# Strassen's product for the output projection of the second layer

## The chip, the cores and the metric

The kernel runs on one core of one Trainium2 chip. TensorE (PE) multiplies matrices, VectorE (DVE), ScalarE (ACT) and GpSimd (POOL) do the elementwise work, and SyncE (SP) issues DMAs. The metric is the device time of one execution in microseconds, as the median of several executions.

## The reference

Two decoder layers over 1024 tokens of width 1024 in float32. The first is a sliding-window attention, the second (HGRN2) a gated linear recurrence. What matters here is the end of the second layer: the recurrence's output `o` (normalised per head and scaled by `gnorm_w`) is multiplied by a SiLU gate, projected by a 1024 x 1024 matrix, normalised by rows, scaled and added to the residual.

```python
o = o.reshape(B, T, REC_WIDTH) * jax.nn.silu(z.astype(jnp.float32))
y = o.astype(h.dtype) @ w_out                    # hgrn2_mixer
...
x = x + rmsnorm(y, post_norm_w[layer])           # reference
```

## The kernel before

Every dense product runs as three matmuls in float32r. Each operand x is split into `hi` and `lo` (hi is x rounded by a copy into float32r, lo = x - hi), and `product` (L189) adds hi x hi, hi x lo and lo x hi into one PSUM tile. Splitting a tile takes one copy (ScalarE, L154 for weights) and one subtraction (DVE, L155).

**Weights** are a stream of 128 x 512 slots. `fetch` (L134) loads a slot into one of four raw buffers `wraw`; `advance` splits it into one of ten places (`whi`, `wlo`) when a place is free; `used` counts a slot's eight reads and frees its place at the last. A DMA into a raw buffer waits for the split of the slot that was there. The splits are emitted under `hp()`, which gives them priority in the order that the compiler's scheduler plans; every engine then works off its instructions in that fixed order.

**Activations** are held feature-major: `act[k, half]` has rows k x 128 to (k+1) x 128 of the features and 512 of the tokens, as `hi` and `lo`.

**The last stage.** `z_unit(c, t)` computes 512 columns of the gate for 128 tokens (24 matmuls: 8 blocks of the contraction by 3) and multiplies the recurrence's output `vo[c]` by it on POOL (L848). `gated(half, ks)` transposes the gated output on PE (L839) and evicts it with `act_from_psum` (L179, L180) straight into `act`. `output1` then runs 16 units of 24 matmuls, column half c outermost, then the 8 token blocks t. Of each PSUM tile ScalarE takes the sum of squares (L885) and DVE the product with `wpost` (L886). With the second half of the columns a row block is finished: `rstd_of` on POOL (L214, L216), two DVE instructions that scale and add the residual `xr`, loaded from `x1d` (L899), and two DMAs to the output (L900). The last unit runs in two halves of 256 columns. PSUM has eight banks under four tags (`mm`, `t`, `s`, `o`, two buffers each).

Of the kernel before, what the change touches and what calls it, by code (L numbers as in the profile page):

```python
# [23 lines left out]
P = 128  # L24
T = 1024
D = 1024
# [6 lines left out]
# rotary frequencies 500000 ** (-j / 8) in float32  # L33
# [34 lines left out]
# rows of a head in the scores' products: rotated dimensions at 0..8 and 32..40  # L68
# [10 lines left out]
class InOrder:  # L79
    """an engine whose instructions keep the program's order while .on is set"""  # L80
# [9 lines left out]
def emit(tc, I, out):  # L90
# [4 lines left out]
    with top:  # L95
# [31 lines left out]
        NS = I["w"].shape[0]  # L127
        W_K = 10
        W = {"split": 0, "fetch": 0, "left": {}, "place": {}, "dmas": {}, "split_ins": {}, "actl": {}, "free": list(zip(whi, wlo))}

        def fetch(end):
            while W["fetch"] < min(end, NS):
                f = W["fetch"]
                W["dmas"][f] = nc.sync.dma_start(wraw[f % NR], I["w"][f])  # L134
                W["fetch"] += 1

        def advance(end=NS):
            """fetch and split the next slots, as far as places are free (in program order)"""
            while W["split"] < end:
                i = W["split"]  # L140
                fetch(i + NR)
# [6 lines left out]
                raw, (hi, lo) = wraw[i % NR], W["place"][i]  # L148
                with hp():
                    on_pool = i in (2, 3)  # L150
# [7 lines left out]
        def used(i):  # L158
            """one of the eight reads of slot i has been emitted"""
            W["left"][i] = W["left"].get(i, 8) - 1  # L160
# [13 lines left out]
        # at first x, then the first heads' attention, then layer 1's first value columns  # L174
# [11 lines left out]
        def product(ps, k, stat, mov):  # L186
            (sh, sl), (mh, ml) = stat, mov
            for i, (a, b) in enumerate(((sh, mh), (sh, ml), (sl, mh))):
                nc.tensor.matmul(ps, a, b, start=(k == 0 and i == 0), stop=(k == NK - 1 and i == 2))  # L189
# [10 lines left out]
        def proj_nat(first, t, c0=0, c1=512, tag="mm"):  # L200
            """token-major [128 tokens, columns c0 to c1 of 512]"""
# [9 lines left out]
        def rstd_of(pool, ms, width, eps=EPS):  # L211
            """(ms + eps) ** -0.5 on [128, width]"""
# [6 lines left out]
        def row_rstd(pool, xt, junk=None):  # L219
            """of the rows of xt (SBUF [128, 1024])"""  # L220
# [6 lines left out]
        def norm_rows(pool, xt, hn, r=None):  # L227
            """rows of xt over their root mean square"""
# [12 lines left out]
        # =====================================================================  # L241
        # layer 0
# [6 lines left out]
        def halves(t):  # L249
            """columns by which the t-th rows of x are taken; the first half's last rows go in two steps"""  # L250
# [8 lines left out]
        def lower_bounds(sp):  # L259
            """layer 1's lower bounds: softmax over the two rows of logits"""  # L260
# [11 lines left out]
        def rope_tables(sp, cosT, sinT, cosK, tK):  # L272
            """rotary tables; the steps to the angles on [(j, chunk), 64], in turns, and what follows them"""
# [6 lines left out]
            def neg_frac(x):  # L280
                """x = round(x) - x, in two steps"""
# [42 lines left out]
        # =====================================================================  # L324
        # layer 0
        def layer0():
            """attention mixer up to its gated output; leaves x + mixer in x1d and its norm in act"""
# [8 lines left out]
            # of 128 keys from 64 before each block, and the last 64 keys twice  # L336
# [126 lines left out]
            with pool("att", "right") as ap:  # L463
                def z_unit(p, half):
                    ps = proj_feat(20 + 2 * (p ^ 4), half)
                    with hp():
# [4 lines left out]
                        # the last heads' last gates come before their attention, the others after  # L471
# [9 lines left out]
                def values_twice(g, b):  # L481
                    """for the blocks b and b + 1, twice: the former block's earlier 64 keys and the block's later ones"""
# [9 lines left out]
                def attn(g, b):  # L492
# [6 lines left out]
                    for par in range(2):  # L499
                        o = par * 64  # L500
                        # scores of the 128 keys a query may see (their slots: see host_arrays), and 8 x the sink
# [7 lines left out]
                        for hp in range(2):  # L509
# [8 lines left out]
                            # the slots of the block's later half and of the former block's earlier half  # L518
# [21 lines left out]
                        # what lies outside of the 128 keys from 64 before the block, hi and lo below each other  # L540
# [482 lines left out]
```

## Time and profile before

| | before |
|---|---|
| runs (us) | 930.67, 934.92, 934.74 |
| median (us) | 934.74 |
| span of the profiled execution (us) | 930.7 |
| busy in it: PE, DVE, ACT, POOL (us) | 902.9, 551.1, 373.6, 355.7 |
| granted TensorE clock, mean | 0.991 |

The profiled execution's own time is its span, 930.7 us, which is the first and lowest of the three runs; nothing of the metric lies outside of it. The median is 4.1 us above. A matmul's busy time is modelled and overlaps the next one's, so distances between units say more of PE than the mean of one. In rows of the timeline the columns are start and duration in us, engine, line, operation, tiles, shapes and count; the square bracket holds idle time of the engine before it and what ended it. "x4" with one duration is four instructions from the first's start to the last's end.

### The profile page before, as it was taken

To read this page: it belongs to the slowest core of one execution; us is meant where nothing else is said; L and a number is where in the kernel's file an instruction comes from. 1 tells how busy PE (TensorE), PEld (TensorE's weight loads), DVE (VectorE), ACT (ScalarE), POOL (GpSimd) and SP (SyncE) were. 2 spreads that over 40 slices of the span, in tenths; PEclk is the share of its full clock that TensorE was granted. 3 is DMA by queue.
4 is the path that set the end of the run, shared out by engine and by line. 5 is a ranking of instruction groups with operands and counts; after the bars stand their busy time and mean duration, and the time that the engine had idled before them with its cause. 6 is when DMAs were issued, how large, how long until landed. Compare 5 with 4: busy or idle time off the path is not lost.

```text
span 930.7 us, 13298 instructions
## 1 busy us (share of the span) xinstructions
PE 902.9 (97%) x4830; PEld 755.8 (81%) x4830; DVE 551.1 (59%) x895; ACT 373.6 (40%) x958; POOL 355.7 (38%) x514
## 2 busy tenths in 40 slices
PE   6989999999999999989999999999999999999996
PEld 5768888888877788768888888888888888888885
DVE  6859888777776436771266855237765835252233
ACT  6425667666666232542332331333233224142210
POOL 6503455667787105450034532114433633220011
PEclk9998999999999999999999999999999999999998
DMA  8455364512311233440311010121111002022053
GB/s 282 141 151 152 107 184 131 162 55 74 86 44 61 86 91 137 137 147 5 110 56 35 24 46 1 38 72 29 45 46 47 1 1 79 12 81 102 24 181 118
DMA packets 53252, 78.56 MB, mean 84 GB/s; under 512 B 4760, under 2 KB 24984, under 8 KB 53176
## 3 DMA queue, kind: packets, MB, share of 16 engines
q1 hardware_dynamic: 53032, 77.51, 27.5%
q8 instruction: 40, 0.66, 0.3%
q14 instruction: 36, 0.29, 0.1%
q10 hardware_dynamic: 144, 0.10, 0.0%
HBM read 58.89 MB, written 16.88 MB: 81 GB/s over the span
## 4 chain that ended last, share of the span: by engine, by line
PE 55%; DVE 3%; POOL 1%; issue 1%; ACT 1%; DMA 1%; ACTq 0%; POOLq 0%
PE psmm L189 46%; PE pso L825 2%; PE pss L769 2%; PE pso L827 1%; PE psk L812 1%; DVE xn L640 1%; PE pss L790 1%; POOL rstd L216 1%; PE pst L839 1%; PE pst L806 1%; ACT jkx L224 1%; DVE xn L639 1%; PE pss L775 1%; DMA wraw<-in_w 1%; DVE actl L180 0%
## 5 line engine op out<-in xcount | busy, mean ns | idle before, releaser
L189 PE MATMUL psmm<-acth,whi 128*128 128x512 f32 x528 | 209.8, 397 | 1.9 <-DVE th L473 1.0
L189 PE MATMUL psmm<-acth,wlo 128*128 128x512 f32 x528 | 208.8, 395 | 0.2 <-POOL wlo L155 0.2
L189 PE MATMUL psmm<-actl,whi 128*128 128x512 f32 x528 | 208.7, 395 | 0.0
L189 PE MATMUL psmm<-whi,acth 128*128 128x512 f32 (+1 forms) x520 | 202.9, 391 | 0.5 <-DVE th L473 0.4
L189 PE MATMUL psmm<-wlo,acth 128*128 128x512 f32 (+1 forms) x520 | 201.9, 389 | 0.2 <-DVE wlo L155 0.2
L189 PE MATMUL psmm<-whi,actl 128*128 128x512 f32 (+1 forms) x520 | 201.6, 389 | 0.0
L155 DVE TENSOR_TENSOR wlo<-wraw,whi 128x512 fp32r<-128x512 f32 x126 | 92.8, 748 | 114.5 <-ACT whi L154 109.6
L189 PEld LDWEIGHTS psmm<-acth,whi 128*128 128x128 f32 x528 | 99.7, 189 | 22.1 <-DVE th L473 2.1
L189 PEld LDWEIGHTS psmm<-acth,wlo 128*128 128x128 f32 x528 | 99.8, 189 | 19.8 <-POOL wlo L155 0.6
L189 PEld LDWEIGHTS psmm<-whi,acth 128*128 128x128 f32 x520 | 98.0, 189 | 20.6 <-DVE th L473 0.9
L189 PEld LDWEIGHTS psmm<-actl,whi 128*128 128x128 f32 x528 | 99.8, 189 | 18.3
L189 PEld LDWEIGHTS psmm<-whi,actl 128*128 128x128 f32 x520 | 98.0, 188 | 20.5 <-DVE actl L592 0.8
L189 PEld LDWEIGHTS psmm<-wlo,acth 128*128 128x128 f32 x520 | 98.1, 189 | 19.9 <-DVE wlo L155 0.6
L154 ACT ACTIVATE whi<-wraw 128x512 fp32r<-128x512 f32 x112 | 70.2, 630 | 86.6 <-PE psmm L189 66.1
L528 ACT ACTIVATE sm<-sm,st 128x129 f32<-128x129 f32 x128 | 50.0, 393 | 51.9 <-DVE st L526 51.9
L681 POOL TENSOR_SCALAR gate<-gate,lbt 128x512 f32<-128x512 f32 x16 | 15.4, 960 | 131.9 <-ACT gate L679 131.9
L886 DVE TENSOR_TENSOR y<-psmm,wpost 128x512 f32<-128x512 f32 (+1 forms) x17 | 11.2, 659 | 52.4 <-ACT jk L885 49.4
L545 POOL TENSOR_SCALAR_AFFINE_SELECT mY<-pT 64x256 fp32r<-64x256 f32 x56 | 29.2, 522 | 31.7 <-ACT pT L537 26.7
L216 POOL TENSOR_TENSOR rstd<-ms,nhalf 128x1 f32<-128x1 f32 (+1 forms) x48 | 38.8, 809 | 3.4
L785 POOL TENSOR_TENSOR kk<-kk,tt 128x512 f32<-128x512 f32 x16 | 24.9, 1556 | 34.6 <-PE pss L775 28.6
L513 PE MATMUL pss<-KH,QS 128*128 128x256 f32 (+1 forms) x128 | 33.4, 288 | 3.5 <-DMA QS<-qd 3.5
L885 ACT ACTIVATE jk<-psmm 128x512 f32<-128x512 f32 (+1 forms) x17 | 9.7, 571 | 65.6 <-PE psmm L189 65.6
(226 smaller groups left out, 1478.2 us busy)
## 6 DMA issues: line engine op xcount, KB each, us to landing
wraw<-in_w SPq DMA_DIRECT2D x132, 256.0 KB
QS<-qd SPq DMA_DIRECT2D x16, 512.0 KB
xr<-in_x SPq DMA_DIRECT2D x8, 512.0 KB
x1d<-xn SPq DMA_DIRECT2D x8, 512.0 KB
xr<-x1d SPq DMA_DIRECT2D x8, 512.0 KB
out_dram<-xn SPq DMA_DIRECT2D x16, 256.0 KB
xh<-in_x SPq DMA_DIRECT2D x4, 512.0 KB
qd<-qh SPq DMA_DIRECT2D x8, 256.0 KB
```

Source lines behind the costliest of these rows:

```text
L154: nc.scalar.activation(hi, raw, AF.Copy)
L155: W["split_ins"][i] = (nc.gpsimd if on_pool else v).tensor_tensor(lo, raw, hi.bitcast(F32), op=ALU.subtract)
L189: nc.tensor.matmul(ps, a, b, start=(k == 0 and i == 0), stop=(k == NK - 1 and i == 2))
L216: W["rstd"] = nc.gpsimd.tensor_tensor(r, m, nhalf[:, :width], op=ALU.pow)
L513: nc.tensor.matmul(ps[:, i, :nkk], q, KH[:, g, k0:k0 + nkk], start=True, stop=False)
L528: nc.scalar.activation(sm[:, h, :], sm[:, h, :], AF.Exp, bias=nm[:, h:h + 1], scale=0.125, accum_out=dn[:, h:h + 1])
L545: nc.gpsimd.affine_select(mY[r, :, :64], src[64:, :, :64].bitcast(F32), [[0, 4], [-1, 64]], ALU.is_gt, 0.0, base=0, channel_multiplier=1)
L681: nc.gpsimd.tensor_scalar(dst, dst, ol, lb, op0=ALU.mult, op1=ALU.add)
L769: nc.tensor.matmul(ps[:, i, :], V[:, cs], U[:, cs], start=True, stop=True)
L785: nc.gpsimd.tensor_tensor(Yv[:, :, 0, :], Yv[:, :, 0, :], tv[:, :, 1:2].to_broadcast([P, nb, n]), op=ALU.mult)
L825: nc.tensor.matmul(po[:, i, :], sc[:, c, :], vt[:, c, hc], start=True, stop=(c == 0))
L886: v.tensor_tensor(y[:, c0:c1], ps, wpost[:, c * 512 + c0:c * 512 + c1], op=ALU.mult)
```

## The change

The projection's two matrices are halved both ways: the gated output A into A11, A12 (first 512 tokens; first and second 512 features) and A21, A22, the weights B into B11, B12 (first 512 features; first and second 512 columns) and B21, B22. In place of eight products of halves there are seven (Winograd's form of Strassen's product), run in this order:

| | left | right | added to |
|---|---|---|---|
| 1 | A11 | B11 | the start of all others; copied to `u2` |
| 2 | A12 | B21 | on the first in PSUM: y11 done |
| 3 | S2 = A22 - S3 | T2 = T3 + B11 | `u2` |
| 4 | S3 = A11 - A21 | T3 = B22 - B12 | with `u2` to `u3` |
| 5 | A22 | T4 = B21 - T2 | on the fourth in PSUM, with `u2`: y21 done |
| 6 | S1 = A21 + A22 | T1 = B12 - B11 | `u3`: y22 done |
| 7 | S4 = A12 - S2 | B22 | on the sixth in PSUM, with `u2`: y12 done |

The weight stream becomes a list of entries, of which one may need no, one, two or three raw tiles; the sums T are formed on POOL ahead of the split. The last 16 entries of eight reads become 28 of four reads, and 16 raw loads become 36. `gated` now evicts into a float32 tile `af` on ScalarE and splits that from SBUF. `sums` and `sums2` form S on POOL and DVE and split them. Row products of `wpost` run on DVE for the first 512 tokens and on POOL for the other 512. The residual rows are loaded ahead into buffers that have come free. The gate units of c = 1 move from the recurrence's pool of buffers to that of the last stage, and `gated` uses two PSUM tags for three. The rest of the kernel is as before; comments are gone.

```diff
+        def strassen_entries(b, tag):
+            f3, f2 = tag + "3", tag + "2"
+            def t2(k, raws):
+                nc.gpsimd.tensor_tensor(W[f3][k], raws[0], raws[1], op=ALU.subtract)
+                nc.gpsimd.tensor_tensor(W[f2][k], W[f3][k], raws[2], op=ALU.add)
+                return W[f2][k]
+            def t4(k, raws):
+                nc.gpsimd.tensor_tensor(W[f2][k], raws[0], W[f2][k], op=ALU.subtract)
+                return W[f2][k]
+            def t1(k, raws):
+                nc.gpsimd.tensor_tensor(W[f3][k], raws[0], raws[1], op=ALU.subtract)
+                return W[f3][k]
+            for i in range(8):
+                entry([b + i], 4)
+            for k in range(4):
+                entry([b + 12 + k, b + 8 + k, b + k], 4, lambda r, k=k: t2(k, r))
+            for k in range(4):
+                entry([], 4, lambda r, k=k: W[f3][k])
+            for k in range(4):
+                entry([b + 4 + k], 4, lambda r, k=k: t4(k, r))
+            for k in range(4):
+                entry([b + 8 + k, b + k], 4, lambda r, k=k: t1(k, r))
+            for k in range(4):
+                entry([b + 12 + k], 4)
...
-                fetch(i + NR)
+                make, r0, r1, reads = ENT[i]
+                fetch(r0 + NR)
...
+                raws, (hi, lo) = [wraw[r % NR] for r in range(r0, r1)], W["place"][i]
                 with hp():
+                    raw = make(raws) if make else raws[0]
...
+            def split(pair, x):
+                nc.scalar.activation(pair[0], x, AF.Copy)
+                v.tensor_tensor(pair[1], x, pair[0].bitcast(F32), op=ALU.subtract)
...
-                    act_from_psum(k, half, pt, cst[:, C_GN:C_GN + 1])
+                    nc.scalar.activation(af[k, half], pt, AF.Copy, scale=cst[:, C_GN:C_GN + 1])
+                    if half == 0 or k >= 4:
+                        split(act[k, half], af[k, half])
+            def sums(k):
+                nc.gpsimd.tensor_tensor(s3[k], af[k, 0], af[k, 1], op=ALU.subtract)
+                v.tensor_tensor(af[k, 0], af[4 + k, 1], s3[k], op=ALU.subtract)
+                split(s2p[k], af[k, 0])
+                split(act[k, 1], s3[k])
+            def sums2(k):
+                nc.gpsimd.tensor_tensor(af[k, 1], af[k, 1], af[4 + k, 1], op=ALU.add)
+                nc.gpsimd.tensor_tensor(af[4 + k, 0], af[4 + k, 0], af[k, 0], op=ALU.subtract)
+                split(act[k, 0], af[k, 1])
+                split(act[4 + k, 0], af[4 + k, 0])
+            def part(ps, left, e, t, more, done=True, cols=(0, 512)):
+                c = slice(t * P, (t + 1) * P)
+                for k in range(4):
+                    hi, lo = left[k]
+                    product(ps, k, (hi[:, c], lo[:, c]), weight(e, k, *cols), None if more else 0, 3)
...
+            banks = ["mm", "mm", "s", "s"]
+            def row_part(c, t, y, x, cs, ss, eng):
+                jk = fp.tile([P, 512], F32, tag="sg", bufs=2, name="jk")
+                nc.scalar.activation(jk[:, :cs.stop - cs.start], y, AF.Square, scale=D ** -0.5, accum_out=ss)
+                eng.tensor_tensor(x, y, wpost[:, c * 512 + cs.start:c * 512 + cs.stop], op=ALU.mult)
+            def finish(t, ss, eps, y0, y1):
+                r = rstd_of(fp, ss, 1, eps)
+                for i, yh in enumerate((y0, y1)):
+                    v.scalar_tensor_tensor(yh, yh, r, xrs[t, i], op0=ALU.mult, op1=ALU.add)
+                    nc.sync.dma_start(out[t * P:(t + 1) * P, i * 512:(i + 1) * 512], yh)
+            def x_rows(t):
+                for i in range(2):
+                    xrs[t, i] = af[4 * i + t, 0] if t < 4 else s2p[t - 4][i].bitcast(F32)
+                    nc.sync.dma_start(xrs[t, i], x1d[t * P:(t + 1) * P, i * 512:(i + 1) * 512])
...
             for t in range(5):
-                z_unit(1, t)
+                z_unit(fp, vo, 1, t)
             gated(0, range(4))
...
+            for t in range(4):
+                p12.append(mm(tag=banks[t]))
+                part(p12[t], quad(0, 0), E[0], t, False)
+                nc.scalar.activation(u2[t], p12[t], AF.Copy)
+                if t < 2:
+                    gated(1, range(4 * t, 4 * t + 4))
+                for k in ((), (), (0, 1), (2, 3))[t]:
+                    sums(k)
+            for t in range(4):
+                part(p12[t], quad(4, 0), E[1], t, True)
...
+                row_part(0, t, p12[t], y, whole, ss, v)
+                add_eps(ss, EPS)
+                ys[t] = y
+            for t in range(4):
+                ps = mm(tag="to"[t % 2])
+                part(ps, s2p, E[2], t, False)
+                v.tensor_tensor(u2[t], ps, u2[t], op=ALU.add)
+                sums2(t)
+            p74 = []
+            for t in range(4):
+                p74.append(mm(tag=banks[t]))
+                part(p74[t], quad(0, 1), E[3], t, False)
+                v.tensor_tensor(u3[t], p74[t], u2[t], op=ALU.add)
+                x_rows(4 + t)
+            for t in range(4):
+                part(p74[t], quad(4, 1), E[4], t, True)
+                x_rows(t)
...
+                v.tensor_tensor(y, p74[t], u2[t], op=ALU.add)
...
+                row_part(0, 4 + t, y, y, whole, ss, nc.gpsimd)
+                add_eps(ss, EPS)
+            p53 = []
+            for t in range(4):
+                p53.append(mm(tag="to"[t % 2]))
+                part(p53[t], quad(0, 0), E[5], t, False)
...
+                v.tensor_tensor(u3[t], p53[t], u3[t], op=ALU.add)
+                ss = ssall[:, 1, 4 + t:5 + t]
+                row_part(1, 4 + t, u3[t], u3[t], whole, ss, nc.gpsimd)
+                finish(4 + t, ss, ssall[:, 0, 4 + t:5 + t], s3[t], u3[t])
+            for t in range(4):
...
+                cuts = [slice(0, 256), slice(256, 512)] if t == 3 else [whole]
+                for cs in cuts:
+                    last = cs.stop == 512
+                    part(p53[t][:, cs], quad(4, 0), E[6], t, True, last, (cs.start, cs.stop))
+                    v.tensor_tensor(u2[t][:, cs], p53[t][:, cs], u2[t][:, cs], op=ALU.add)
...
+                    row_part(1, t, u2[t][:, cs], u2[t][:, cs], cs, ss, v)
...
+                finish(t, ss, eps, ys[t], u2[t])
```

More of the change, by code (lines that the diff above doesn't have):

```diff
@@ L158, in used @@
         def used(i):
-            W["left"][i] = W["left"].get(i, 8) - 1
+            W["left"][i] = W["left"].get(i, ENT[i][3]) - 1
             if W["left"][i] == 0:
@@ L184, in mm, with product @@
             return pp.tile(list(shape), F32, tag=tag, name="psmm")
-        def product(ps, k, stat, mov):
+        def product(ps, k, stat, mov, first=0, last=NK - 1):
             (sh, sl), (mh, ml) = stat, mov
             for i, (a, b) in enumerate(((sh, mh), (sh, ml), (sl, mh))):
-                nc.tensor.matmul(ps, a, b, start=(k == 0 and i == 0), stop=(k == NK - 1 and i == 2))
+                nc.tensor.matmul(ps, a, b, start=(k == first and i == 0), stop=(k == last and i == 2),
+                                 skip_group_check=first is None)
         def proj_feat(first, half):
@@ new lines, in sums2 @@
+            def sums2(k):
[8 more added lines that the diff above has]
+                    product(ps, k, (hi[:, c], lo[:, c]), weight(e, k, *cols), None if more else 0, 3)
+                    if done:
+                        used(e + k)
@@ new lines, in final1 @@
+            quad = lambda k0, half: [act[k0 + k, half] for k in range(4)]
+            E = [E_OUT1 + 4 * i for i in range(7)]
+            banks = ["mm", "mm", "s", "s"]
+            ys, xrs = {}, {}
+            def row_part(c, t, y, x, cs, ss, eng):
+                jk = fp.tile([P, 512], F32, tag="sg", bufs=2, name="jk")
+                nc.scalar.activation(jk[:, :cs.stop - cs.start], y, AF.Square, scale=D ** -0.5, accum_out=ss)
+                eng.tensor_tensor(x, y, wpost[:, c * 512 + cs.start:c * 512 + cs.stop], op=ALU.mult)
@@ L859, in mixer1 @@
+            whole = slice(0, 512)
             for t in range(5):
[L860 removed]
+                z_unit(fp, vo, 1, t)
             gated(0, range(4))
[L862 removed]
+            z_unit(fp, vo, 1, 5)
             gated(0, range(4, 8))
[L864 to L906 removed]
```

117 lines of the change are left out of this document (55 added, 62 removed).

## The prediction

> **What bounds the kernel now.** The page's totals come first, then a table by stage, then the chain that ended last.
>
> ```profile
> span 930.7 us, 13298 instructions
> ...
> PE 902.9 (97%) x4830; PEld 755.8 (81%) x4830; DVE 551.1 (59%) x895; ACT 373.6 (40%) x958; POOL 355.7 (38%) x514
> ```
>
> ```profile
> core 0: us, PE busy (x) PEld busy (x) DVE busy (x) ACT busy (x) POOL busy (x), PEclk, DMA share, GB/s
> 831.50:840.50 9.00, 9.00 (x58) 7.99 (x57) 5.82 (x9) 6.81 (x13) 1.51 (x2) 1.00 0.86 246
> 840.50:857.00 16.50, 16.50 (x74) 13.63 (x74) 4.71 (x7) 2.72 (x8) 0.38 (x2) 1.00 0.25 101
> 857.00:890.00 33.00, 33.00 (x147) 27.32 (x146) 9.46 (x14) 8.11 (x19) 1.76 (x7) 1.00 0.13 37
> 890.00:911.50 21.50, 21.50 (x96) 17.83 (x95) 8.43 (x12) 2.49 (x9) 3.23 (x8) 1.00 0.58 193
> 911.50:931.00 19.50, 10.94 (x71) 9.84 (x70) 6.48 (x10) 2.17 (x8) 2.68 (x7) 0.83 0.29 108
> ```
>
> ```profile
> 824.96 6.58 PE psmm L189 x29
> 831.53 1.75 PE pst L839 x16
> 833.28 5.47 PE psmm L189 x24
> 838.75 1.75 PE pst L839 x16
> 840.50 81.95 PE psmm L189 x384
> ```
>
> PE is busy 97% of the span. In the stage that is changed it never pauses, at a granted clock of 1.00, while DVE, ACT and POOL stand nearly idle: from 840.5 to 911.5 (71 us) DVE works 4.71 + 9.46 + 8.43 = 22.6 us and POOL 5.4 us. The chain is PE alone: the last gate unit ends at 831.53, and transposes, the first output unit, transposes and the other 15 units take 90.92 us to 922.45. So shorter PE work shortens the time one for one, as long as the idle engines really have room for what is put on them.
>
> **What is removed from PE.** One output unit is 24 matmuls; ScalarE squares each as it ends, so the distance of two squares is a unit.
>
> ```profile
> 851.51 0.60 ACT L885 ACTIVATE jk<-psmm 128x512 f32<-128x512 f32 x1 [4.75 <-PE psmm L189]
> ...
> 856.95 0.60 ACT L885 ACTIVATE jk<-psmm 128x512 f32<-128x512 f32 x1 [4.75 <-PE psmm L189]
> ...
> 919.66 0.39 ACT L885 ACTIVATE jk<-psmm 128x256 f32<-128x256 f32 x1 [2.19 <-PE psmm L189]
> ...
> 922.48 0.38 ACT L885 ACTIVATE jk<-psmm 128x256 f32<-128x256 f32 x1 [2.34 <-PE psmm L189]
> ```
>
> A unit is 5.44 us, so 12 matmuls (half the contraction) are 2.72; 24 narrow matmuls are 2.82, so 12 are 1.41. After: seven products of four blocks of 12, the very last block in two narrow halves: 27 x 2.72 + 2 x 1.41 + 2 x 1.75 of transposes = 79.8 us for 90.9. PE loses 11.1 us and would end at 911.3.
>
> **The end behind PE.** Before, DVE ends at 925.46 and the span 5.25 us later, when the last rows have landed.
>
> ```profile
> 922.98 0.42 DVE L886 TENSOR_TENSOR y<-psmm,wpost 128x256 f32<-128x256 f32 x1 [2.39 <-ACT jk L885]
> 924.04 1.42 DVE L899 SCALAR_TENSOR_TENSOR xn<-y,rstd,xr 128x512 f32<-128x512 f32 x2 [0.63 <-POOL rstd L216]
> ```
>
> From PE's end to DVE's it is 3.01 us. The change puts one more DVE addition (U2 onto PSUM, 0.43) in front of the last square: 3.44. If PE stays the bound the span is 911.3 + 3.44 + 5.25 = 920.0, 10.7 less. This is the floor.
>
> **What is added to DVE and POOL.** I number the seven products A to G (10.9 us each on PE; A has 3.5 us of transposes more). From 840.5 on, when the last transposes are done and the left operand sums can start, DVE gets, in instructions of 512 columns:
> - A and B (to about 857): 4 `lo` splits of `gated`, 12 in `sums` (4 subtractions, 8 splits), 4 weight splits of T2 and 2 of T3, 3 row products: 25
> - C: 1 row product, 4 additions to U2, 8 splits of `sums2`, 4 weight splits: 17
> - D and E: 4 additions and 4 weight splits each: 16
> - F: 4 additions, 2 weight splits, 8 of `finish`; G: 4 additions and 4 row products (with the halves), 8 of `finish`: 30
>
> That is 88, 16 of them `finish`. Of these 24 read PSUM, and 64 have both inputs in SBUF. POOL gets 34 sums or products of 512 columns from that point: 6 of T2 (2 are earlier), 4 of S3, 4 of T4, 4 of T1, 8 in `sums2`, 8 row products of units 4 to 7. Their prices:
>
> ```profile
> 833.97 0.68 DVE L847 TENSOR_TENSOR sg<-psmm,sg 128x512 f32<-128x512 f32 x1
> 834.57 0.68 DVE L155 TENSOR_TENSOR wlo<-wraw,whi 128x512 fp32r<-128x512 f32 x1
> ...
> 874.60 2.69 DVE L155 TENSOR_TENSOR wlo<-wraw,whi 128x512 fp32r<-128x512 f32 x4
> ```
>
> ```profile
> 820.45 1.29 POOL L848 TENSOR_TENSOR vo<-vo,sg 128x512 f32<-128x512 f32 x1 [4.83 <-PE pst L839]
> 827.65 1.67 POOL L848 TENSOR_TENSOR vo<-vo,sg 128x512 f32<-128x512 f32 x1 [5.91 <-DVE sg L847]
> ```
>
> Two DVE instructions follow each other after 0.60 us; a pair of `finish` takes 1.42, 0.67 to the next. So DVE's own work is 72 x 0.605 + 16 x 0.67 = 54.3 us, which would fit in PE's 71 us. But the two engines hold each other up. The first fence is DVE, the second POOL, at the same moments:
>
> ```profile
> 359.23 1.67 DVE L640 TENSOR_TENSOR xn<-xn,xr 128x512 f32<-128x512 f32 x1
> 360.82 0.68 DVE L615 TENSOR_TENSOR y<-psmm,bout 128x512 f32<-128x512 f32 x1
> ...
> 802.91 1.45 DVE L180 SCALAR_TENSOR_TENSOR actl<-pst,cst,acth 128x512 fp32r<-128x512 f32 x2
> ...
> 827.47 3.60 DVE L155 TENSOR_TENSOR wlo<-wraw,whi 128x512 fp32r<-128x512 f32 x4
> ```
>
> ```profile
> 358.61 1.73 POOL L640 TENSOR_TENSOR xn<-xn,xr 128x512 f32<-128x512 f32 x1 [0.87 <-DVE xn L639]
> ...
> 803.14 1.30 POOL L848 TENSOR_TENSOR vo<-vo,sg 128x512 f32<-128x512 f32 x1 [4.30 <-PE psmm L189]
> ```
>
> Four splits took 2.69 us alone and 3.60 beside one POOL product: 0.91 lost. The addition at 359.23 held DVE for 1.59 (to the next start) where 0.605 is usual: 0.99 lost. The two instructions at 802.91, which read PSUM, lost nothing (1.45). So a POOL sum costs DVE between 0 (DVE in a PSUM instruction or idle) and 0.99 us. Most of DVE's instructions from 840.5 are of the kind that loses: 64 of 88. I take 0.95 x 64/88 = 0.69, or 34 x 0.69 = 23.5 us. DVE's queue then has 54.3 + 23.5 = 77.8 us of work from 840.5, more than PE's 70.8 to 911.3: **DVE, not PE, sets the end**. By stages: 25 x 0.605 + 10 x 0.69 = 22.0 us of work in the 16.3 that PE leaves for A and B (5.7 late); C 15.1 and D with E 18.7 in 32.7 (6.8 late); F and G 22.0 in 21.8, so DVE ends 7.0 behind PE, where 3.4 cannot be avoided. To 840.5 + 77.8 = 918.3 I add 1.2 for the start, when DVE's first work waits for ScalarE (two instructions of 0.6), and 0.5 at the end: `finish` now comes every 2.72 us, so four output rows of 256 KB are under way where two were. With 5.25 to land this is 925.3, **5.4 less than 930.7**.
>
> The Trainium skill (SBUF — State Buffer, "Who interferes with whom") states that a VectorE instruction with two SBUF inputs contends with a GpSimd instruction that reads SBUF, as an exclusive lock held for the whole instruction. By that a POOL sum would cost its full 1.30 whenever DVE wants such an instruction, 1.30 x 64/88 = 0.95 in the mean, and the sum would be 934 instead of 925.3, slower than before. The two rows here, 0.91 and 0.99, are below 1.30, so the trace agrees with a lock but not with the whole instruction's length.
>
> **What waits for the late engines.** PE in C needs T2 and S2. T2 takes three raw tiles for one, and only four raw buffers exist.
>
> ```profile
> 828.19 7.42 SPq L134 DMA_DIRECT2D wraw<-in_w  x7
> ```
>
> ```profile
> 831.68 0.63 ACT L154 ACTIVATE whi<-wraw 128x512 fp32r<-128x512 f32 x1 [2.15 <-DMA wraw<-in_w]
> 832.69 0.63 ACT L154 ACTIVATE whi<-wraw 128x512 fp32r<-128x512 f32 x1 [0.39 <-DMA wraw<-in_w]
> ```
>
> A tile asked for at 828.19 is there at 831.68, 3.5 us later, the next 1.0 behind. Each T2 tile waits once for a freed buffer, so four take about 4 x (3.5 + 1.3) = 19 us from 837: done at 856, ScalarE and DVE split by 857.5, wanted at 858.8 (C's first block, fourth k). S2's last split stands behind 14 us of DVE and 7 of POOL's interference and comes at about 861: PE waits some 2 us there. I cost that at nothing beyond DVE's sum, since DVE works on meanwhile; if DVE is not the bound it is 2 us on PE. In POOL's queue S3's sums stand behind T2's sums, which wait for DMAs; that is the same wait. ACT has about 24 instructions of 0.63 and 3 squares of 0.8 in A and B, 17.5 us for 16.3: as full, but with slack from C on. In D and E the SP queue issues 16 residual loads of 256 KB, earlier than before, beside 12 weight tiles: 7.3 MB in 21.8 us, 337 GB/s, where the first stage above moved 246. They spill by up to 8 us into F, whose rows need only D's loads; free, unless the weights of the last products stand behind them, at up to 3 us. `wpost` and the gate units' buffers change pool only: nothing. The gates' first half splits through SBUF (8 more ScalarE copies of 0.63) under gate units that keep PE full: nothing, and 5 us if PE had to wait for them.
>
> **The rivals.**
> 1. PE stays the bound: POOL and DVE mostly miss each other. For it: DVE alone is 54.3 for 70.8. Against: A and B are overfull even at half the interference (15.1 + 3.5 for 16.3). It gives 920.0 to 922 on the profile's scale, 924 to 926 against the median.
> 2. The gain is used up: loss of 0.85 per POOL sum, the point at which DVE's path gives 930.7 (840.5 + 54.3 + 1.2 + 0.5 + 5.25 = 901.75; 28.95 / 34). 932 to 937 against the median.
> 3. Slower: every POOL sum meets a DVE instruction with two SBUF inputs. Place: DVE's queue from S2's sums on. Price: 34 x 0.99 = 33.7, so 935.4, or 4.7 above before; it decides from 0.85 on. Against it: the 24 PSUM instructions that lose nothing. Some 939.5 against the median. The lock of the Trainium skill's SBUF page is this mechanism; held for all of 1.30 at every sum it would make 946.
>
> **How the numbers follow.** The sum stands against the profiled span, 930.7, which is also the lowest of the three times; the median is 934.74, 4.0 above. I predict the median: 934.7 - 5.4 = 929.3. Chances: the forecast (gain of 2.5 to 8) 0.40, rival 1 0.26, rival 2 0.19, rival 3 0.15. Half a per cent, 4.7 us, is about what a measurement can tell from no change. Faster by more: rival 1 and a little over half of the forecast, 0.48; slower by more: most of rival 3, 0.14; same: 0.38. The forecast alone spans 926.5 to 932.5. The range reaches from rival 1 in an execution as quick as the quickest before (920.0) nearly, 921.5, to rival 3, 939.5.
>
> **What would show it.** Right: 336 full-width matmuls' worth in the stage, PE's last one near 911 to 915; DVE over 80% busy from 845 to the end; two-input DVE instructions at a mean of 0.9 us and more, POOL's sums at 1.5 and more; PE waiting 1 to 3 us before C on S2 or T2; four to seven us from PE's end to DVE's. Wrong: DVE idle in D and E (rival 1), PE waiting in several products (rivals 2 and 3), or a DMA as releaser of a weight split in E to G.

## The result, and the profile after

The changed kernel takes 945.66 us in the median (943.48 to 946.47, four runs) where the kernel before took 932.70 beside it (930.63 to 934.92, four runs). The ratio is 1.0134 [1.0108, 1.0161]: **1.3% slower**. The forecast was 929.3 with a range up to 939.5, so both were wrong.

In the page of the profile after, the totals changed as the edit says (60 matmuls fewer, 41 DVE and 36 POOL instructions more), and yet the span is 13.4 us longer and PE's share of it lower:

```profile
span 944.1 us, 13386 instructions
...
PE 898.9 (95%) x4770; PEld 750.5 (79%) x4770; DVE 600.7 (64%) x936; ACT 397.6 (42%) x1002; POOL 415.2 (44%) x550
```

Next come the table by stage, with the columns that were shown of before, and PE's waits from 826 on (total us, times, longest). Before, every stretch from 840 to 911 had PE fully busy at a clock of 1.00.

```profile
core 0: us, PE busy (x) PEld busy (x) DVE busy (x) ACT busy (x) POOL busy (x), PEclk, DMA share, GB/s
850.00:860.00 10.00, 3.86 (x17) 2.84 (x16) 10.00 (x7) 7.17 (x15) 10.00 (x7) 0.79 0.27 80
860.00:870.00 10.00, 6.52 (x16) 4.87 (x17) 10.00 (x8) 3.73 (x10) 9.79 (x8) 0.67 0.24 81
870.00:880.00 10.00, 9.41 (x35) 7.20 (x34) 10.00 (x14) 5.04 (x10) 3.92 (x4) 0.85 0.15 52
880.00:890.00 10.00, 10.00 (x45) 8.10 (x44) 6.14 (x10) 1.90 (x3) 5.60 (x4) 1.00 0.85 294
```

```profile
PE psmm L232 <- DVE s2l L915: 7.1, 1, 7.1
PE psmm L232 <- DVE u L1037: 4.5, 1, 4.5
PE psmm L232 <- DVE wlo L198: 3.1, 2, 2.6
```

From 850 to 870 DVE and POOL are both busy all of the time, and DVE gets through only 15 instructions of 512 columns in 20 us. PE stands and its clock falls. From 880 on PE is full again, up to the last block. PE's timeline has the places (all of its rows are start, duration, and in brackets the idle time and who ended it):

```profile
853.46 0.40 PE L232 MATMUL psmm<-wlo,s2h 128*128 128x512 f32 x1
860.92 0.79 PE L232 MATMUL psmm<-whi,s2l 128*128 128x512 f32 x1 [7.07 <-DVE s2l L915]
861.51 0.63 PE L232 MATMUL psmm<-whi,acth 128*128 128x512 f32 x1
...
865.78 0.55 PE L232 MATMUL psmm<-wlo,acth 128*128 128x512 f32 x1
...
866.40 0.40 PE L232 MATMUL psmm<-whi,s2h 128*128 128x512 f32 x1
869.35 0.67 PE L232 MATMUL psmm<-wlo,s2h 128*128 128x512 f32 x1 [2.56 <-DVE wlo L198]
...
927.11 0.28 PE L232 MATMUL psmm<-whi,actl 128*128 128x256 f32 x1
931.91 0.58 PE L232 MATMUL psmm<-whi,acth 128*128 128x256 f32 x1 [4.52 <-DVE u L1037]
```

PE waits 7.5 us (from start to start) for the first split of S2, 3.0 us for a weight split of T2, and 4.8 us between the two halves of the very last block. Behind the first wait the matmuls are 0.43 us apart, where 0.227 is usual; PE works off a block of product 2 (`acth`) that its fixed order has put behind the first matmuls of product 3 (`s2h`).

**The balance.** I call "PE's stage" the time from the first transposes of `gated` to PE's last matmul. It was 831.37 to 922.44 before, 91.1 us; it is 833.30 to 934.83 after, 101.5 us. The three waits are 14.6 us of that (7.2 + 2.7 + 4.7, less one usual step each); without waits the stage takes 80.7 (fin_b below), so 6.2 us are a smaller gap and the lower clock. That last part is what is left over, not a reading of its own. The rest of the 13.4 us: 1.9 because the stage starts later in this profile (the other changed kernels start it anywhere from 828.0 to 833.2, so this is put down to the spread of single profiles, see the last section), and 1.0 in the tail.

### The profile page after: what moved, and what is told of

It reads as the page before. It is cut to its first block, busy times and chain, and to the rows that moved or that the text cites. A ratio compares the mean times of both kernels' runs of the same rounds, so it can differ in the third digit from the quotient of the medians.

```text
span 944.1 us, 13386 instructions
## 1 busy us (share of the span) xinstructions
PE 898.9 (95%) x4770; PEld 750.5 (79%) x4770; DVE 600.7 (64%) x936; ACT 397.6 (42%) x1002; POOL 415.2 (44%) x550
## 4 chain that ended last, share of the span: by engine, by line
PE 48%; DVE 6%; POOL 3%; issue 2%; ACT 2%; DMA 1%; ACTq 0%; POOLq 0%; DVEq 0%
PE psmm L232 39%; PE pso L869 2%; PE pss L813 2%; PE pso L871 1%; PE psk L856 1%; POOL rstd L260 1%; DVE xn L684 1%; PE pss L834 1%; DMA wraw<-in_w 1%; ACT jkx L268 1%; POOL ms L258 1%; DVE actl L915 1%; PE pst L921 1%; PE pst L850 1%; DVE xn L683 1%
## 5 line engine op out<-in xcount | busy, mean ns | idle before, releaser
L232 PE MATMUL psmm<-whi,acth 128*128 128x512 f32 (+1 forms) x484 | 192.3, 399 | 5.0 <-DVE u L1037 4.5
L232 PE MATMUL psmm<-wlo,acth 128*128 128x512 f32 (+1 forms) x484 | 190.7, 395 | 0.4 <-DVE wlo L198 0.4
L232 PE MATMUL psmm<-whi,actl 128*128 128x512 f32 (+1 forms) x484 | 190.4, 395 | 0.0
L232 PEld LDWEIGHTS psmm<-whi,acth 128*128 128x128 f32 x484 | 92.9, 192 | 24.2 <-DVE u L1037 4.7
L232 PEld LDWEIGHTS psmm<-whi,actl 128*128 128x128 f32 x484 | 92.7, 192 | 19.8 <-DVE actl L636 0.8
L232 PEld LDWEIGHTS psmm<-wlo,acth 128*128 128x128 f32 x484 | 93.0, 192 | 19.5 <-DVE wlo L198 0.9
L197 ACT ACTIVATE whi<-wraw 128x512 fp32r<-128x512 f32 x108 | 67.6, 629 | 83.1 <-PE psmm L232 69.1
L589 POOL TENSOR_SCALAR_AFFINE_SELECT mY<-pT 64x256 fp32r<-64x256 f32 x56 | 29.3, 523 | 32.0 <-ACT pT L581 27.0
L592 POOL TENSOR_SCALAR_AFFINE_SELECT mY<-pT 64x256 fp32r<-64x256 f32 x64 | 30.9, 483 | 6.0 <-ACT pT L581 1.4
L558 PE MATMUL pss<-KL,QS 128*128 128x256 f32 (+1 forms) x128 | 32.9, 284 | 0.0
```

The lines of the kernel that those rows point to most:

```text
L197: nc.scalar.activation(hi, raw, AF.Copy)
L232: nc.tensor.matmul(ps, a, b, start=(k == first and i == 0), stop=(k == last and i == 2), skip_group_check=first is None)
L558: nc.tensor.matmul(ps[:, i, :nkk], q, KL[:, g, k0:k0 + nkk], start=False, stop=True)
L589: nc.gpsimd.affine_select(mY[r, :, :64], src[64:, :, :64].bitcast(F32), [[0, 4], [-1, 64]], ALU.is_gt, 0.0, base=0, channel_multiplier=1)
L592: nc.gpsimd.affine_select(mY[r, :, 64:], src[:64, :, 64:].bitcast(F32), [[0, 4], [1, 64]], ALU.is_ge, 0.0, base=0, channel_multiplier=-1)
```

## What DVE and POOL do to each other

The first fence is DVE's timeline of the kernel after, the second its DVE groups from 842 to 871 us, the third POOL's groups in the same window (busy us, mean ns).

```profile
855.77 1.75 DVE L930 TENSOR_TENSOR af<-vo,o 128x512 f32<-128x512 f32 x1
857.44 1.75 DVE L915 TENSOR_TENSOR actl<-vo,acth 128x512 fp32r<-128x512 f32 x1
859.12 1.75 DVE L915 TENSOR_TENSOR s2l<-af,s2h 128x512 fp32r<-128x512 f32 x1
...
869.22 0.68 DVE L915 TENSOR_TENSOR actl<-vo,acth 128x512 fp32r<-128x512 f32 x1
869.82 0.68 DVE L198 TENSOR_TENSOR wlo<-o,whi 128x512 fp32r<-128x512 f32 x1
870.42 0.68 DVE L915 TENSOR_TENSOR s2l<-af,s2h 128x512 fp32r<-128x512 f32 x1
```

```profile
L930 DVE TENSOR_TENSOR af<-vo,o 128x512 f32<-128x512 f32 x4 | 6.9, 1774 | 0.0
L915 DVE TENSOR_TENSOR actl<-o,acth 128x512 fp32r<-128x512 f32 x4 | 6.2, 1550 | 2.0 <-ACT acth L914 1.9
L915 DVE TENSOR_TENSOR actl<-vo,acth 128x512 fp32r<-128x512 f32 x4 | 5.9, 1486 | 0.0
L915 DVE TENSOR_TENSOR s2l<-af,s2h 128x512 fp32r<-128x512 f32 x4 | 5.9, 1492 | 0.0
L198 DVE TENSOR_TENSOR wlo<-o,whi 128x512 fp32r<-128x512 f32 x3 | 3.5, 1176 | 4.9 <-ACT whi L197 4.9
```

```profile
L936 POOL TENSOR_TENSOR o<-o,vo 128x512 f32<-128x512 f32 x4 | 6.9, 1725 | 0.0
L937 POOL TENSOR_TENSOR af<-af,af 128x512 f32<-128x512 f32 x4 | 6.8, 1719 | 0.0
L929 POOL TENSOR_TENSOR o<-af,o 128x512 f32<-128x512 f32 x4 | 6.0, 1518 | 0.0
L142 POOL TENSOR_TENSOR o<-wraw,wraw 128x512 f32<-128x512 f32 x3 | 5.2, 1732 | 0.0
L143 POOL TENSOR_TENSOR o<-o,wraw 128x512 f32<-128x512 f32 x2 | 3.5, 1738 | 0.0
```

The two engines take turns: a DVE instruction each 1.68 us, a POOL sum each 1.7 us. As soon as POOL has no sum to do (869.2 to 871), DVE is back at one each 0.60. So in this stretch a POOL sum costs DVE 1.68 - 0.60 = 1.08 us. In the window 19 DVE instructions took 28.4 us where 19 x 0.68 = 12.9 is usual: 15.5 us lost beside 17 POOL sums.

That was a reading; three explanations could make S2 and T2 late. **Turns**: POOL's sums take the time from DVE. **DVE's load**: DVE simply has too much to do, and POOL's help is a relief. **POOL's order**: POOL works off all eight of `sums2`'s sums (L936, L937) ahead of T2's last (L143), so what PE wants first comes last, as POOL's timeline shows. (A fourth, the order that the compiler's scheduler gives PE's own work, comes up with all_dve.)

```profile
851.88 3.42 POOL L936 TENSOR_TENSOR o<-o,vo 128x512 f32<-128x512 f32 x2
...
865.35 1.73 POOL L937 TENSOR_TENSOR af<-af,af 128x512 f32<-128x512 f32 x1
...
872.81 1.74 POOL L143 TENSOR_TENSOR o<-o,wraw 128x512 f32<-128x512 f32 x1
```

## The experiments

All ratios are to the kernel before in the same runs, with 95% intervals. "Behind" is DVE's end after PE's, "to the end" the span's end minus the stage's start; the last three columns are from one profile of each.

| kernel | ratio | PE's stage (us) | behind | to the end |
|---|---|---|---|---|
| before | 1 | 91.1 | 3.0 | 99.3 |
| after | 1.0134 [1.0108, 1.0161] | 101.5 | 3.8 | 110.8 |
| floor | 0.9946 [0.9919, 0.9974] | 84.8 | 3.7 | 93.5 |
| s_dve | 1.0085 [1.0057, 1.0114] | 95.8 | 3.8 | 104.2 |
| no_t | 1.0047 [1.0015, 1.0079] | 95.0 | 3.7 | 104.7 |
| order | 1.0155 [1.0111, 1.0199] | 104.0 | 3.7 | 112.5 |
| banks | 1.0086 [1.0056, 1.0116] | 95.8 | 8.9 | 110.0 |
| all_dve | 0.9907 [0.9882, 0.9932] | 83.2 | 4.6 | 93.0 |
| best | 0.9921 [0.9901, 0.9942] | 80.7 | 7.5 | 93.0 |
| idle2 | 1.0030 [1.0011, 1.0049] | 92.9 | 4.6 | 102.2 |
| idle1 | 0.9913 [0.9892, 0.9935] | 83.7 | 4.1 | 92.7 |
| fin_b | 0.9893 [0.9877, 0.9909] | 80.7 | 5.2 | 90.5 |
| fin_a | 0.9917 [0.9901, 0.9932] | 80.7 | 6.2 | 91.7 |

**floor**: the seven products with no sums to wait for.

```diff
-                entry([b + 12 + k, b + 8 + k, b + k], 4, lambda r, k=k: t2(k, r))
+                entry([b + k], 4)      # all sums T likewise: one raw tile each
...
             def sums(k):               # sums2 likewise
-                nc.gpsimd.tensor_tensor(s3[k], af[k, 0], af[k, 1], op=ALU.subtract)
...
+                pass
```

> Left out: all operand sums S and T; the seven products take plain quarters of the operands, so the result is not the projection. 28 blocks of 12 matmuls, evictions, row products and loads stay. All theories: with the sums and their splits gone nothing keeps PE waiting before the last block; PE's stage takes 80 to 82 us and the span is 920 to 924 (the floor of the prediction, 920.0, and up to 2 us that this kind of execution loses at the start of layer 1). If it stays above 930, the loss is not in the sums at all but in the finer stream of weights or in the order of the last stage.

PE's only wait is 3.6 us, ahead of the last twelve matmuls. Without it the stage of 84.8 us would be 81.2, near the 79.8 that was worked out: the seven products do save what they should, and the loss before the last block is made by the sums or their splits, which are both left out here. That last wait appears here too, so it is not made by the sums.

**s_dve**: the 12 left sums moved from POOL to DVE. DVE gets more to do.

```diff
-                nc.gpsimd.tensor_tensor(s3[k], af[k, 0], af[k, 1], op=ALU.subtract)
+                v.tensor_tensor(s3[k], af[k, 0], af[k, 1], op=ALU.subtract)
...          (both sums of sums2 likewise)
```

> The 12 left sums (S3, S1, S4) run on DVE in place of POOL; nothing else. Theory 'lock' (a POOL sum and a DVE instruction with two SBUF inputs take turns, 1.69 us for a pair where DVE alone needs 0.605): DVE takes 12 x 0.6 = 7 us more work and loses 12 x 1.08 = 13 us fewer, S2 comes 5 us earlier and T2 no longer stands behind sums: 931 to 936. Rival 'DVE load' (DVE simply has too much): 7 us more, 948 to 952. Rival 'order' (T2's sums stand behind sums2 in POOL's queue): T2 is free, 931 to 936 as well; the run 'order' tells these two apart.

PE's waits of this kernel:

```profile
PE psmm L232 <- DVE s2l L915: 5.1, 1, 5.1
PE psmm L232 <- DVE u L1037: 5.0, 1, 5.0
PE psmm L232 <- ACT u L988: 0.8, 1, 0.8
```

More work on DVE made its results earlier: the wait on S2 is 2 us shorter, the one on T2 is gone, and the stage is 5.7 us shorter. That speaks against DVE's load. The intervals of the two ratios barely overlap.

**no_t**: the sums T left out, their splits kept; T3's place gets a raw tile of its own, four loads more.

```diff
-                entry([b + 12 + k, b + 8 + k, b + k], 4, lambda r, k=k: t2(k, r))
+                entry([b + 12 + k, b + 8 + k, b + k], 4, lambda r, k=k: r[2])
...
```

> Left out: the 16 sums T of the weights on POOL (the raw tile is split instead; result not the projection). The 12 left sums stay on POOL. 'Lock': 8 POOL sums fewer in products A and B, DVE gains 8 x 1.08 = 8.6 us there, 928 to 934. 'Order': nothing of the weights stands in POOL's queue, 926 to 932, DVE's two-input instructions still at 1.7 us beside sums. 'DVE load': DVE's own instructions are the same, 942 to 946.

The wait on weights falls to 0.2 us and the one on S2 from 7.1 to 4.3. S2 does not use T, so T's sums held S2 up, on POOL's queue or by their turns; this run does not say which. Its 935.08 us lie above what "lock" and "order" gave and below "DVE load".

**order**: `sums2`'s POOL sums queued behind T2's last sum.

```diff
+                with tc.issue_after(W["t2"].ins):
-                nc.gpsimd.tensor_tensor(af[k, 1], af[k, 1], af[4 + k, 1], op=ALU.add)
+                    nc.gpsimd.tensor_tensor(af[k, 1], af[k, 1], af[4 + k, 1], op=ALU.add)
...
```

> The eight POOL sums of sums2 are queued behind the last sum of T2 (an edge in the planned order); no work is added or removed. 'Order': T2 is ready 8 to 10 us earlier, PE's wait before C goes, 930 to 936. 'Lock': the same number of locks falls on the same splits; T2 comes earlier but S2's splits still alternate with POOL sums at 1.69 us and PE waits on s2l as before (7 us of the 15): 938 to 943. 'DVE load': no change, 944.

```profile
PE psmm L232 <- DVE wlo L198: 5.1, 3, 2.7
PE psmm L232 <- DVE s2l L915: 4.5, 1, 4.5
PE psmm L232 <- DVE u L1038: 4.2, 1, 4.2
```

What S2's wait lost (2.6 us), the weights' wait gained (2.0), and the ratio is that of the kernel after. POOL's order decides who is late, not how late all are: the third explanation is not the cause of the loss.

**all_dve**: every sum and row product of the change on DVE, none on POOL.

```diff
-                nc.gpsimd.tensor_tensor(W[f2][k], W[f3][k], raws[2], op=ALU.add)
+                v.tensor_tensor(W[f2][k], W[f3][k], raws[2], op=ALU.add)
...          (all other sums likewise)
-                row_part(0, 4 + t, y, y, whole, ss, nc.gpsimd)
+                row_part(0, 4 + t, y, y, whole, ss, v)
...
```

> All sums S and T and all row products on DVE, POOL has only its small column instructions; DVE has 36 instructions of 0.605 us, 21.8 us, more than in the changed kernel and no lock. 'Lock': DVE loses 36 x (1.08 - 0.605) = 17 us less than with POOL's help; DVE's own 54.3 + 20.6 = 75 us still exceed PE's 71, A and B are overfull (22 to 24 us of work for 16.3), so PE waits 4 to 6 us before C: 926 to 931, better than with 12 sums moved (933.8). 'DVE load': 22 us more work on the fullest engine, 950 or more.

Its table by stage, at the same places:

```profile
850.00:860.00 10.00, 10.00 (x45) 8.19 (x44) 10.00 (x17) 9.31 (x22) 7.81 (x3) 1.00 0.42 130
860.00:870.00 10.00, 10.00 (x45) 8.12 (x44) 10.00 (x18) 1.04 (x3) 1.91 (x2) 1.00 0.79 263
```

DVE is as busy as before (10.00 of 10), but does 35 instructions in the 20 us where the kernel after did 15, and PE never waits there. With 36 instructions more in DVE's queue the kernel goes from 1.3% slower to 0.9% faster than before. DVE's load as the cause is refuted. The wait of 4 to 6 us before product 3 that was expected even here did not come.

One thing besides the sums differs: the compiler's scheduler orders PE's work anew for each kernel. In the kernel after, PE's first stretch of product 3 is 3 matmuls long and two blocks of product 2 stand behind it; in all_dve that stretch is 32 long. So these two kernels alone do not tell the turns from the order. The next two do.

**idle2 and idle1**: all_dve and 12 needless POOL instructions from product 1 on, whose results nobody uses. In idle2 they read two tiles, in idle1 one.

```diff
             def sums(k):
+                for _ in range(3):     # idle2
+                    nc.gpsimd.tensor_tensor(scr, af[4 + k, 1], wpost[:, :512], op=ALU.subtract)
...
+                for _ in range(3):     # idle1
+                    nc.gpsimd.tensor_scalar(scr, af[4 + k, 1], 1.0, 1.0, op0=ALU.mult, op1=ALU.mult)
```

> The kernel with all sums on DVE, and 12 needless POOL subtractions of 512 columns with two SBUF inputs beside products A and B, whose results nobody reads; DVE's and PE's own work stays. 'Lock': DVE loses up to 1.08 us at each, 13 us in a stage where it is already full, so S2 and T2 come 8 to 13 us later and PE stands before C: 931 to 936 in the profile where it was 923.4. 'Order' or any theory by which POOL's sums only hurt when something waits for their results: 923 to 925.

> The same with 12 needless POOL instructions of 512 columns with one SBUF input (scale by 1). The Trainium skill's rule (a lock against every GpSimd instruction that reads SBUF) makes them cost their own length, at 0.7 us alone about 0.6 each, 7 us: 928 to 931. If only POOL's two-input instructions hold DVE up: 923 to 925.

Here no result passes between POOL and DVE in the sums, and the planned order is the same: from the stage's start, PE's 380 rows and DVE's 129 come in one sequence in both profiles, and PE's in all_dve as well. So the price stands alone. (One tie is left: DVE later overwrites tiles that the needless instructions read, and idle1's DVE waits 0.7 us for that.) idle2 took 934.37 us in the median, idle1 924.78, in the same runs. The rows are idle2's: its needless sums (duration min, median, max in ns), then POOL's timeline, then DVE's.

```profile
L932 POOL TENSOR_TENSOR scr<-vo,wpost x12: 1607/1620/17501, 840.4 to 876.8; 128x512 f32<-128x512 f32 x12
```

```profile
840.43 27.68 POOL L932 TENSOR_TENSOR scr<-vo,wpost 128x512 f32<-128x512 f32 x7 [7.26 <-ACT vo L923]
```

```profile
856.10 0.68 DVE L147 TENSOR_TENSOR o<-wraw,o 128x512 f32<-128x512 f32 x1
856.70 0.68 DVE L963 TENSOR_TENSOR vo<-psmm,wpost 128x512 f32<-128x512 f32 x1
857.30 1.17 DVE L915 TENSOR_TENSOR s2l<-af,s2h 128x512 fp32r<-128x512 f32 x1
858.40 1.77 DVE L915 TENSOR_TENSOR actl<-o,acth 128x512 fp32r<-128x512 f32 x1
860.10 1.78 DVE L915 TENSOR_TENSOR s2l<-af,s2h 128x512 fp32r<-128x512 f32 x1
```

From 858.4 on DVE's instructions with two SBUF inputs take 1.77 and start 1.70 apart: the turns, with no result passing between the engines to explain them. DVE is late in consequence, and PE waits for it where it did not in all_dve, though at another place than was expected. Its waits for weight splits are only 1.7 us, and there is none for S2, two of whose four splits were done before the first needless sum came in. The long one is for DVE's additions to `u2`, which follow product 3:

```profile
PE psmm L232 <- DVE u L1008: 5.2, 1, 5.2
```

idle2's span of 930.2 us is just under the 931 to 936 expected for it.

The 12 instructions with one input cost nothing that shows (idle1 against all_dve: 0.9913 and 0.9907). Its needless instructions, and DVE in the midst of them:

```profile
L932 POOL TENSOR_SCALAR scr<-vo x12: 617/1118/16980, 843.6 to 881.8; 128x512 f32<-128x512 f32 x12
```

```profile
859.99 0.69 DVE L963 TENSOR_TENSOR vo<-psmm,wpost 128x512 f32<-128x512 f32 x1
...
861.18 0.69 DVE L915 TENSOR_TENSOR actl<-o,acth 128x512 fp32r<-128x512 f32 x1
861.79 0.69 DVE L915 TENSOR_TENSOR s2l<-af,s2h 128x512 fp32r<-128x512 f32 x1
```

These instructions did meet DVE's, and lost. The first took 17.0 us where the shortest took 0.62, and it ended at 860.55, beside the DVE instruction of 859.99, which reads PSUM. Eleven of the twelve ended beside such a DVE instruction, the last in a gap of DVE. So idle1 does not show that one-input instructions keep clear of DVE: they got in only where DVE lost nothing by it. Whether DVE is spared because they have one input or because they are short (0.62 where a sum takes 1.29 alone) no run tells, since idle1 changes both.

The first explanation is shown: a POOL sum of two SBUF operands takes the time from DVE's instructions of that kind, whether or not anybody wants its result.

**banks**: in the last block, products 6 and 7 get a PSUM tile for each half, as the kernel before had; in the change both halves share one.

```diff
-                p53.append(mm(tag="to"[t % 2]))
...
+                    p53.append([mm((P, 256), tag) for tag in ("mm", "s")])   # t == 3
...
-                    part(p53[t][:, cs], quad(4, 0), E[6], t, True, last, (cs.start, cs.stop))
+                    pk = p53[t] if t < 3 else p53[t][cs.start // 256]
+                    part(pk, quad(4, 0), E[6], t, True, last, (cs.start, cs.stop))
```

> Only the last block of products F and G is changed: its two column halves get a PSUM tile each instead of halves of one tile. Theory 'bank': in every kernel so far PE waits 3.8 to 6.9 us before the very last 12 matmuls, because they write the bank that DVE still has to read for the first half; with two tiles this wait is gone and PE ends 4 to 5 us earlier: 939 to 942 in the profile where the changed kernel had 944.1. The rest behind it (DVE's queue is late by itself) may take back up to 3 of them. Rival: the wait is for DVE's queue anyhow and the end does not move, 944.

PE's wait at the end is gone, and its stage is 5.8 us shorter, but DVE ends 8.9 us behind PE where 3.8 were: in the profile only 0.8 us reach the end. The times say more, 940.57 in the median and a ratio lower by 0.5%, with intervals that overlap by a little. With the turns gone (all_dve against fin_b) the same edit takes 2.5 us off stage and tail in one profile of each, and the intervals of the two ratios overlap. The wait is real, its worth between 1 and 5 us is not settled closer.

**best, fin_b, fin_a**: what is the best version? All have the two PSUM tiles. fin_b is all_dve with them. best instead forms T2 and T3 on POOL early, under the gate units, and the left sums on DVE; T4, T1 and row products stay on POOL. fin_a is best with the row products on DVE.

```diff
+            for k in range(4):                       # best, fin_a: T3 and T2 under the gate units
+                raw = [af[k, 0], af[4 + k, 0], u2[k]]
+                for x, j in zip(raw, (128 + k, 124 + k, 116 + k)):
+                    nc.sync.dma_start(x, I["w"][j])
+                nc.gpsimd.tensor_tensor(W["o13"][k], raw[0], raw[1], op=ALU.subtract)
+                nc.gpsimd.tensor_tensor(W["o12"][k], W["o13"][k], raw[2], op=ALU.add)
```

> T2 and T3 are formed early: their 12 raw tiles are loaded into buffers of the last stage that are still empty and POOL adds them under the gate units, where DVE has little to do; the 12 left sums run on DVE; the last block has two PSUM tiles. T4, T1 and four-row products stay on POOL. 'Lock': in A and B no POOL sum is left, DVE has 29 x 0.605 = 17.5 us of work for 16.3, so PE waits at most 2 us before C; later 16 POOL sums meet a DVE that has room; PE's stage 80 to 83 us, span 920 to 925, faster than before by 6 to 10 us. If S2's chain or the stream's DMAs are the true cause, PE still waits 5 us before C and the span stays above 927.

> All sums and row products on DVE and two PSUM tiles for the last block. PE's last wait (2.4 us) goes; DVE ends 4.6 us behind PE in the run without it and works through a queue there, so at most 2 us come back: 921 to 923.4.

> T2 and T3 early on POOL under the gate units, left sums and all row products on DVE, T4 and T1 on POOL, two PSUM tiles for the last block. PE has no waits as in the run 'best'; DVE ends 3.5 to 4.5 us behind PE in place of 7.5, since no POOL row product stands before POOL's rstd and no sum locks the last additions: 920 to 923.

In all three PE has no wait in the stage and needs 80.7 us. They differ in what is left behind PE: 7.5 us in best, 6.2 in fin_a and 5.2 in fin_b, in the order in which POOL has less to do; that POOL's work is the reason was not tested. best's span (926.2, expected 920 to 925) and fin_a's 6.2 us (expected 3.5 to 4.5) missed. The span from fin_b's page:

```profile
span 919.9 us, 13401 instructions
```

**fin_b beats both kernels**: 921.97 us in the median, 0.9893 [0.9877, 0.9909] of before, with no sum of the change on POOL at all. POOL's help at the sums T2 and T3, at a time when DVE has few such instructions (best, fin_a), gains nothing more.

## Why the prediction was wrong

- **What PE saves** was right. The working gave 79.8 us for the stage; best, fin_a and fin_b need 80.7, and before needed 91.1.
- **DVE's own work** was right in its price: without POOL's sums DVE's instructions start 0.60 apart. The sum's end is no proof of more: with the 34 sums that all_dve adds (34 x 0.605 = 20.6) it gives 917.1, and all_dve's DVE ended at 918.2, but that closeness is partly luck. DVE stood idle for 5 us on the way, and its end follows PE's by 4.6.
- **The price of a POOL sum** was mis-sized. I had 0.95 for a meeting and took 64/88 of it, 0.69, because 24 of DVE's 88 instructions read PSUM. But those 24 come mostly from product 3 on. From 842 to 871 all 19 of DVE's are of the losing kind, and a meeting in step costs 1.08. The forecast had ten sums beside products 1 and 2, at 6.9 us; the profile has 17 beside the 19 instructions up to 871, and they lost 15.5, since POOL ran ahead of DVE into the sums that I had counted for product 3. S2's last split, forecast at 861, ended at 871.1 (the row at 870.42).
- **"I cost that at nothing beyond DVE's sum, since DVE works on meanwhile"** is the step that failed worst. I summed DVE's queue over the whole stage, as if lateness in product 3 could be made good in products 4 to 7, where DVE has slack. But PE takes its instructions in order: the 7.5 and 3.0 us that it stood are lost for good, and with them the lower clock behind. DVE is then partly idle (6.14 of 10 busy from 880 to 890) in the slack that I had counted on. The stage must be summed product by product, and PE's loss is the largest lateness, not the last.
- **The halves of the last block** were costed at 2 x 1.41 alone. In the change they share a PSUM tile, and the second half of product 7 stands until DVE has read the first (931.44 in DVE's queue, 4.1 us after the first half's last matmul):

```profile
931.44 0.42 DVE L1037 TENSOR_TENSOR u<-psmm,u 128x256 f32<-128x256 f32 x1
```

- **Rival 3** was the right mechanism and nearly the right place ("from S2's sums on"); I gave it 0.15 and 939.5. Its price of 0.99 was near the 1.08, and PSUM instructions, which spoke against it, came too late to help. What it lacked is PE's wait: its 935.4 on the profile's scale was 944.1.
- **The Trainium skill** (SBUF — State Buffer, "Who interferes with whom") was the better guide than my average. The sentence that I read against the trace, an exclusive lock for a whole instruction, would make the price 1.30; measured is 1.08 in step. That its 946 us (on the profile's scale, where 944.1 was measured) comes close is chance: it too was a sum over DVE's queue. The same section says that a VectorE instruction with two SBUF inputs contends with a GpSimd instruction that reads SBUF. idle1's trace agrees: its instructions have one input and still stood up to 17.0 us. There the loss fell on POOL alone, so what this case adds is which of the two pays.
- **What would show it**: DVE over 80% busy from 850 to 930 (mean 8.3 of 10), POOL's sums over 1.5 and DVE's over 0.9 us came as forecast, though from standing in turns. PE waiting in several products was named as the sign of rivals 2 and 3, and came. DVE idle in products 4 and 5, the sign of rival 1, came in part too (7.30 of 10 busy from 900 to 910), so it told nothing apart; PE's last matmul near 911 to 915 did not come.
- Residual loads (326 GB/s at most) and the later weights made PE wait nowhere; that was right.

Open: how the 15.5 us divide between T's and S's sums (no_t and s_dve each took away about half of PE's waits for S2 and T2), what the bank at the end is worth with the turns in place, and what PE's planned order adds in the kernel after. When S2's last split came at 871.1, one block of product 2 (12 matmuls) was still to do; had it stood ahead of product 3, that would have saved its 2.7 us at most (an estimate from 12 x 0.227; no run has it).

## What to carry to other kernels

An idle engine is not free help when the helped one is what it slows: moving the sums to the busier engine made the kernel 2.2% faster. Price such a meeting at what the nearest rows show in the stretch where it happens, not at a mean over the stage. And where an in-order engine consumes the results, add up lateness at each point of use; slack after that point gives nothing back.

## What the runs showed of the hardware

- **Turns, and being shut out.** While DVE ran two-input instructions back to back (0.60 apart), idle2's first POOL sum did not come in at all: it took 17.5 us, from 840.4 until after DVE's first instruction that reads PSUM, at 856.70. From then on both alternated, 1.70 us a pair. In the kernel after, DVE had waited for ScalarE at the stage's start, and the turns began at once. Being shut out is not the rule: in that kernel a sum of 871.35 took only 1.50 us, though DVE had run four such instructions 0.60 apart just before it. What decides stays open.
- **The loss can fall on either.** idle1's POOL instructions stretched to 17.0 us at most (0.62 at the shortest), while DVE kept to 0.60. idle2's sums took 1.62 in the turns where 1.29 is usual alone, and DVE's instructions 1.77 where 0.68 is usual.
- **The clock.** After the 7.5 us wait, matmuls came 0.43 us apart for 4.3 us; after the 3.0 us wait, for 3.5 us. The Trainium skill (TensorE: Matmul & The Clock Gate, "Part 1: The HAM clock gate") states that an idle window of some 3.4 us halves the clock. The first wait agrees; the second was shorter than that and was enough.
- **Spread ahead of the stage.** The stage began between 828.0 and 833.3 us in these profiles. Part of it is one DVE instruction of 128 x 1024 (`hn`, L229 before, L273 after) at 409 us, which runs beside POOL's fills of memory: 3.19 us before, 4.09 after. It is 3.19 in floor and banks too and 4.08 in the other changed kernels, so it does not go with the sums; why it differs stays open. A single profile's span carries this; the ratios average over several executions.
